# Attention steps of an encoder block: squares issued before the hi/lo split, small softmax steps on GpSimd, softmax scaling on ScalarE

## The chip, the cores and the metric

One core of a Trainium2 chip runs the kernel. The metric is the time of one launch on the device in microseconds; several runs give a median. One further execution is recorded by the hardware profiler, and the numbers of views come from it. The engines are PE (TensorE, matmuls), DVE (VectorE), ACT (ScalarE), POOL (GpSimd) and SP (SyncE, which here issues DMAs). Each works through its own list of instructions in order, and engines wait for each other through semaphores.

## The reference

One encoder layer over 256 tokens of width 2048, in float32. What matters here is the first half:

```
h = rmsnorm(x)
[q | k | v | u] = h @ w_in
# 12 query heads in 4 groups of 3, head width 128, window |t-s| <= 128
scores = q k^T * 128**-0.5 + alibi(slope of the head, |t-s|)
m = max(max_s scores, sink);  p = exp(scores - m)
p = p / (sum_s p + exp(sink - m));   a = p @ v
f = per group: Re(DFT2(u)) @ w_fourier
x = x + concat(rmsnorm(a), rmsnorm(f)) @ w_out
```

A feed-forward part with a width-3 convolution, GELU and a down-projection follows, and a final RMS norm. Nothing in it is touched.

## The kernel before

**Precision.** Every float32 factor is split into a coarse part (hi, made by a copy on ACT) and the rest (lo, a subtraction on DVE). A product is then three matmuls: hi by hi, hi by lo, lo by hi. Each weight tile of 128 x 2048 is split this way in `split` (lines 174 to 184), and the activations in `split_scaled` (267 to 272) and similar lines.

**Order.** The schedule is written out by hand: instructions stand on each engine in the order in which the Python code issues them. `unit(i, work)` (line 382) is one weight tile. It issues what is put `before` tile i (matmuls of the attention), the tile's own matmuls (`work`), what is put `beside` it (work of ACT, DVE and GpSimd on earlier results), then `split(i + 2)`, which makes the halves of the tile after next and issues the DMA that loads a further raw tile, then what is put `behind`. So TensorE runs tile i while ACT and DVE go through one round: the `beside` work, the split, the `behind` work. Three pairs of hi and lo buffers and three raw buffers rotate.

**Tiles.** Units 0 to 3 make u (for the Fourier part), 4 to 7 make v, 8 to 23 make the four key heads and twelve query heads in the order k, q, q, q (`QK_ORDER`), and 24 to 39 are the output projection. The feed-forward part has its own loop.

**Attention.** The loop of lines 762 to 791 spreads the steps of a head over the rounds. For the tile of slot s, in the round of unit
- s + 1: `qk_out` adds the two halves of the projection (`tmp` on ACT, `add` on DVE, for a key also a product with `r1b`), and `qk_parts` splits the sum into hi (ACT) and lo (DVE), the tiles `qT` and `kT`;
- s + 2: `scores` (six matmuls into `ps_s`, at the start of TensorE's part), then `scores_out` on DVE (add the distances and take the row maximum in one custom operation for each half; two steps on 128 x 2 elements give `neg`), and behind the split `exps` on ACT (exponentials with their row sums `sm`, and `ex`, the sink's term);
- s + 3: `weigh` (add the sink's term, reciprocal, scale the rows) and `flip_out` for the first ten heads (a 32 x 32 block transpose on DVE into `flip`, four DMAs on SP to `turnp` in HBM);
- s + 4: `flip_in`, the DMA back into `flop`; for the last two heads TensorE transposes instead (`turn`, `turn_out`);
- s + 6: `flip_parts`, hi and lo of the transposed weights (`pt`);
- s + 7 (s + 5 for the last two heads): `values` (six matmuls into `ps_o`) and `values_out`.

`values_out` and the Fourier part's last step call `feature_out`: it splits the scaled result into hi and lo (tile `cat`, the input of the output projection) and squares the unscaled result for the later RMS norm. The first square goes straight into the sum (`sq_a` or `sq_f`), the later ones into a scratch tile that GpSimd adds to it. GpSimd has little else in this stretch. The names `ps_...` are PSUM tiles; GpSimd takes no part with these.

In the round of unit i the order on each engine before the change is, where all steps occur:

```
ACT: pt hi | tmp | cat hi | square | kT/qT hi | split hi | exponentials, ex
DVE: pt lo | sm, reciprocal, 2 scalings | transpose | add | cat lo | kT/qT lo
     | 2 reductions, 2 neg steps | split lo
```

Of the kernel before, what the change touches and what calls it, by code (L numbers as in the profile page):

```python
# [8 lines left out]
F32 = mybir.dt.float32  # L9
F32R = mybir.dt.float32r  # L10
AF = mybir.ActivationFunctionType
ALU = mybir.AluOpType

P = 128
D = 2048
S = 256
# [88 lines left out]
def block_kernel(  # L105
# [19 lines left out]
    nc = tc.nc  # L125
# [3 lines left out]
    wp = ctx.enter_context(tc.tile_pool(name="wp", bufs=1))  # L129
# [3 lines left out]
    def f32(ap):  # L133
        return ap.bitcast(F32)

    def bank(pool, name):
        return pool.tile([P, 512], F32, tag=pool.name, name=name)
# [79 lines left out]
    def u_part(k, o, n, m=1):  # L217

        rows = ux[k // 4][:, (k < 4) * U_HEAD :].rearrange("p (k c) -> p k c", k=4)
        return rows[:, k % 4 : k % 4 + m, o : o + n]  # L220
# [39 lines left out]
    ps = bank(dn, "ps_warm")  # L260
# [3 lines left out]
    def vcol(o, n=1):  # L264
        return vec[:, o : o + n]

    def split_scaled(dst, src, g):

        nc.scalar.activation(dst[:, 0:S], src, AF.Copy, scale=g)
        nc.vector.scalar_tensor_tensor(  # L270
            dst[:, S : 2 * S], src, g, f32(dst[:, 0:S]), ALU.mult, ALU.subtract
        )
# [100 lines left out]
    before, beside, behind = {}, {}, {}  # L373

    def at(when, i, f, *a):
        when.setdefault(i, []).append((f, a))
# [17 lines left out]
    for k in range(NK):  # L394
# [7 lines left out]
        if q % n == 0:  # L402
            w, h = u_part(k, 0, FW, n), hi[:, q : q + n, :]
# [26 lines left out]
    rq_neg = ph.tile([P, 2], F32, tag="rq_neg", name="rq_neg")  # L430
    rq_pos = ph.tile([P, 2], F32, tag="rq_pos", name="rq_pos")
    rq_inv = ph.tile([P, 2], F32, tag="rq_inv", name="rq_inv")
    sink_neg = ph.tile([P, NH], F32, tag="sink_neg", name="sink_neg")
# [46 lines left out]
    def feature_out(ps, slot, g, sq, first):  # L480

        t = cat_pool.tile([P, 512], F32R, tag="cat", name=f"cat{slot}")
        split_scaled(t, ps, g)
        cat[slot] = t
        if first:
            nc.scalar.activation(sq, ps, AF.Square)
        else:
            one = wp.tile([P, 512], F32, tag="junk", name=f"sq{slot}")[:, 0:S]
            nc.scalar.activation(one, ps, AF.Square)
            nc.gpsimd.tensor_tensor(sq, sq, one, ALU.add)  # L490

    sums, r_af = {}, {}
# [91 lines left out]
    def fourier_channels_out(g):  # L584
        feature_out(held.pop(("y", g)), NH + g, vcol(V_GF + g), sq_f, g == 0)
# [43 lines left out]
    def qk_out(kind, h, ps):  # L629
        tmp = ph.tile([P, S], F32, tag="tmp", name=f"tmp_{kind}{h}", bufs=2)  # L630
        nc.scalar.activation(tmp, ps[:, S : 2 * S], AF.Copy)
        add = ph.tile([P, S], F32, tag="add", name=f"add_{kind}{h}", bufs=2)
        nc.vector.tensor_tensor(add, ps[:, 0:S], tmp, ALU.add)
        if kind == "k":
            nc.vector.tensor_tensor(add, add, r1b, ALU.mult)
        st["add", kind, h] = add
# [25 lines left out]
    def scores_out(h):  # L662

        ps = st.pop(("s", h))
        sc = ph.tile([P, 512], F32, tag="sc", name=f"sc{h}", bufs=4)
        mx = ph.tile([P, 2], F32, tag="mx", name=f"mx{h}", bufs=2)
        neg = ph.tile([P, 2], F32, tag="neg", name=f"neg{h}", bufs=2)
        for b in range(2):
            s = slice(b * S, (b + 1) * S)
            nc.vector.tensor_tensor_reduce(  # L670
                sc[:, s], ps[:, s], rel[:, s], -float(SL[h]), -3e38, ALU.add,
                ALU.max, mx[:, b : b + 1],
            )
        nc.vector.tensor_tensor(neg, mx, rq_neg, ALU.mult)
        nc.vector.tensor_scalar(neg, neg, sink_neg[:, h : h + 1], None, ALU.min)
        st["sc", h] = sc, neg

    def exps(h):
        sc, neg = st["sc", h]
        sm = ph.tile([P, 2], F32, tag="sm", name=f"sm{h}", bufs=2)  # L680
        ex = ph.tile([P, 2], F32, tag="ex", name=f"ex{h}", bufs=2)
        for b in range(2):
            s = slice(b * S, (b + 1) * S)
            nc.scalar.activation(
                sc[:, s], sc[:, s], AF.Exp, scale=rq_pos[:, b : b + 1],
                bias=neg[:, b : b + 1], accum_out=sm[:, b : b + 1],
            )
        nc.scalar.activation(ex, neg, AF.Exp, bias=vcol(V_SINK + h))
        st["sc", h] = sc, sm, ex

    def weigh(h):
        sc, sm, ex = st["sc", h]
        nc.vector.tensor_tensor(sm, sm, ex, ALU.add)
        nc.vector.reciprocal(ex, sm)
        for b in range(2):
            s = slice(b * S, (b + 1) * S)
            nc.vector.tensor_scalar(sc[:, s], sc[:, s], ex[:, b : b + 1], None, ALU.mult)

    def turn(h):
        ps = st["t", h] = bank(dn, f"ps_t{h}")  # L700
# [56 lines left out]
    def values_out(h):  # L757
        feature_out(st.pop(("o", h))[:, 0:S], h, vcol(V_GA + h), sq_a, h == 0)
# [3 lines left out]
    for i in range(N_QK, N_OUT + 8):  # L762
        heads = {i - s: h for (kind, h), s in slot_of.items() if kind == "q"}
        new = [kh for kh, s in slot_of.items() if i - s == 1]
        for n, h in sorted(heads.items()):
            if n == 5 + 2 * (h in FLIPS):
                at(before, i, values, h)
        if 4 in heads and heads[4] not in FLIPS:
            at(before, i, turn, heads[4])
        if 2 in heads:  # L770
            at(before, i, scores, heads[2])
        if 6 in heads and heads[6] in FLIPS:
            at(beside, i, flip_parts, heads[6])
        if 3 in heads:
            at(beside, i, weigh, heads[3])
            if heads[3] in FLIPS:
                at(beside, i, flip_out, heads[3])
        if 4 in heads and heads[4] in FLIPS:
            at(beside, i, flip_in, heads[4])
        for kind, h in new:  # L780
            at(beside, i, lambda k=kind, h=h: qk_out(k, h, st.pop(("ps", k, h))))
        for n, h in sorted(heads.items()):
            if n == 5 + 2 * (h in FLIPS):
                at(beside, i, values_out, h)
        if 4 in heads and heads[4] not in FLIPS:
            at(beside, i, turn_out, heads[4])
        for kind, h in new:
            at(beside, i, qk_parts, kind, h)
        if 2 in heads:
            at(beside, i, scores_out, heads[2])  # L790
            at(behind, i, exps, heads[2])

    fourier_channels_steps()
# [84 lines left out]
    for n, (c, kq) in enumerate(OUT_ORDER):  # L878
        i = N_OUT + n
# [14 lines left out]
        if kq >= 2:  # L894
            part = "a" if kq == 2 else "f"
            ps = ps_a[c] if kq < 3 else ps_a[c, "f"]
# [315 lines left out]
    for q in range(2):  # L1212
        kind, j = items[q]
        ps = bank(mm, f"ps_{kind}{j}")
# [15 lines left out]
    for n, it in enumerate(items):  # L1230
# [8 lines left out]
        if it[0] in ("gate", "val"):  # L1239
            kind, j = it  # L1240
            ps = bank(mm, f"ps_{kind}{j}")
# [4 lines left out]
        if it[0] == "product":  # L1246
# [4 lines left out]
            elif end and p in ("P2", "N4"):  # L1251
                ps = joined[c, p] = bank(mm, f"ps_{p}{g}{c}")
                by_parts(ps, parts[p], *halves.pop(it), GROUPS[g][1], True, False)
            else:
                ps = bank(mm, f"ps_{p}{g}{c}")
# [5 lines left out]
        else:  # L1261
            kind, c = it
            hi, lo = halves.pop(up_index[n])
            if c < 2:
                ps = [joined.pop((c, p)) for p in ("P2", "N4")]
            else:
                ps = [bank(mm, f"ps_l{c}{b}") for b in range(2)]
# [10 lines left out]
    i = up_index[n]  # L1278
# [37 lines left out]
    junk = wp.tile([P, 512], F32, tag="junk", name="junkc31")[:, 0:256]  # L1316
# [120 lines left out]
```

## Time and profile before

| | us |
|---|---|
| runs: median (lowest to highest) | 946.17 (945.48 to 946.81) |
| the profiled execution, its own time | 944.83 |
| its span in the trace | 943.0 |
| idle of ACT ahead of squares, waiting for DVE | 24.9 in 11 waits, 2.8 in one more |
| GpSimd busy | 50.8 |
| split of one weight tile: hi on ACT, lo on DVE | 1.90, 2.29 |

The profiled execution's time is 1.8 us more than its span: what lies before the first and after the last instruction. A line of a group or a timeline names the engine, the line of the kernel, the operation, output and inputs without buffer numbers, and the shapes; in brackets stands the idle time just before the instruction and what ended it. In the chain that ended last, each line is a start, a length and a piece of work; a piece that has been split over several lines is written as one. L697 DVE is a scaling, L314 the block transpose, L740 `pt` lo, L182 and L181 the split's lo and hi. Waits that are marked with another instruction's name are inferred from semaphores.

### The profile page before, as it was taken

How to read it: one execution, taken by the hardware profiler on the slowest of the kernel's cores; microseconds unless marked ns; L12 is line 12 of the kernel's file. 1: busy time of each engine (PE TensorE's matmuls, PEld its weight loads, DVE VectorE, ACT ScalarE, POOL GpSimd, SP SyncE). 2: the span in 40 equal slices, each digit the busy share in tenths (PEclk: the TensorE clock that was granted, in tenths of full speed). 3: DMA queues.
4: the chain of work that ended last, by engine and by line, in shares of the span. 5: the costliest groups of instructions: out<-in, count | busy, mean ns of one | idle time of the engine just before them, and what ended most of it. 6: DMA issues, size and time to landing. Idle time of an engine off the chain costs nothing.

```text
span 943.0 us, 12851 instructions
## 1 busy us (share of the span) xinstructions
PE 930.6 (99%) x5005; PEld 805.6 (85%) x5005; DVE 771.4 (82%) x981; ACT 540.5 (57%) x672; POOL 50.8 (5%) x68
## 2 busy tenths in 40 slices
PE   9999989999999999999999999999999999999996
PEld 7888878888888888888888888888888888888885
DVE  7658788777777878799887997878988779989986
ACT  7755566645554564566555565555655556655553
POOL 0100000100000000000000000000000000000002
PEclk9999989999999999999999999999999999999998
DMA  9965766566766578877798769787787878779652
GB/s 364 310 224 168 225 200 190 191 209 248 259 229 206 183 238 245 269 250 235 250 272 254 243 230 284 241 265 228 260 247 239 301 240 266 226 236 277 201 179 89
DMA packets 55149, 223.26 MB, mean 237 GB/s; under 512 B 21136, under 2 KB 25744, under 8 KB 31536
## 3 DMA queue, kind: packets, MB, share of 16 engines
q1 hardware_dynamic: 50544, 192.94, 56.6%
q0 software_dynamic: 4544, 29.49, 16.7%
q8 instruction: 39, 0.64, 0.3%
q14 instruction: 22, 0.18, 0.1%
HBM read 216.13 MB, written 6.29 MB: 236 GB/s over the span
## 4 chain that ended last, share of the span: by engine, by line
PE 88%; DVE 5%; ACT 4%; issue 2%; DMA 1%; DVEq 0%; SPq 0%; POOLq 0%; POOL 0%; ACTq 0%
PE ps_val L350 25%; PE ps_gate L350 25%; PE ps_P L1148 3%; PE ps_P L1146 3%; PE ps_P L1147 3%; PE ps_N L1148 3%; PE ps_N L1147 3%; PE ps_N L1146 3%; PE ps_a L335 2%; PE ps_a L334 2%; PE ps_a L333 2%; ACT hi L181 2%; DVE lo L182 1%; PE ps_ff L333 1%; PE ps_ff L335 1%
## 5 line engine op out<-in xcount | busy, mean ns | idle before, releaser
L182 DVE TENSOR_TENSOR lo<-raw,hi 128x2048 fp32r<-128x2048 f32 (+1 forms) x129 | 293.4, 2274 | 46.4 <-ACT hi L181 43.7
L181 ACT ACTIVATE hi<-raw 128x2048 fp32r<-128x2048 f32 (+1 forms) x129 | 245.2, 1901 | 34.2 <-PE ps_a L334 14.4
L350 PE MATMUL ps_val<-hU,hi 128*128 128x512 f32 x688 | 236.2, 389 | 0.0
L350 PE MATMUL ps_gate<-hU,hi 128*128 128x512 f32 x688 | 236.2, 389 | 0.0
L350 PE MATMUL ps_val<-hU,lo 128*128 128x256 f32 x688 | 189.9, 276 | 0.0
L350 PE MATMUL ps_gate<-hU,lo 128*128 128x256 f32 x688 | 189.9, 276 | 0.0
L350 PEld LDWEIGHTS ps_gate<-hU,hi 128*128 128x128 f32 x688 | 129.2, 188 | 26.8
L350 PEld LDWEIGHTS ps_val<-hU,hi 128*128 128x128 f32 x688 | 129.1, 188 | 26.8
L350 PEld LDWEIGHTS ps_gate<-hU,lo 128*128 128x128 f32 x688 | 129.2, 188 | 1.3
L350 PEld LDWEIGHTS ps_val<-hU,lo 128*128 128x128 f32 x688 | 129.2, 188 | 1.3
L921 ACT ACTIVATE ft_g<-ps_gate 128x256 f32<-128x256 f32 x43 | 16.5, 384 | 123.1 <-PE ps_gate L350 123.1
L921 ACT ACTIVATE ft_v<-ps_val 128x256 f32<-128x256 f32 x43 | 16.5, 384 | 91.8 <-PE ps_val L350 91.8
L350 PE MATMUL ps_q<-hT,hi 128*128 128x512 f32 x192 | 67.2, 401 | 0.0
L1146 PE MATMUL ps_P<-hi_P,op_P 128*128 128x512 f32 x144 | 56.0, 389 | 0.0
L1147 PE MATMUL ps_P<-hi_P,op_P 128*128 128x512 f32 x144 | 56.0, 389 | 0.0
L1148 PE MATMUL ps_P<-lo_P,op_P 128*128 128x512 f32 x144 | 56.0, 389 | 0.0
L350 PE MATMUL ps_q<-hT,lo 128*128 128x256 f32 x192 | 52.0, 281 | 0.0
L1038 DVE TENSOR_TENSOR lo_N<-sumw,hi_N 128x2048 fp32r<-128x2048 f32 (+1 forms) x20 | 41.5, 2076 | 9.4 <-ACT hi_N L1037 9.2
L350 PEld LDWEIGHTS ps_q<-hT,hi 128*128 128x128 f32 x192 | 36.3, 194 | 7.0
L1146 PE MATMUL ps_N<-hi_N,op_N 128*128 128x512 f32 x108 | 42.0, 389 | 0.0
L1147 PE MATMUL ps_N<-hi_N,op_N 128*128 128x512 f32 x108 | 42.0, 389 | 0.0
L1148 PE MATMUL ps_N<-lo_N,op_N 128*128 128x512 f32 x108 | 42.0, 389 | 0.0
(389 smaller groups left out, 1584.7 us busy)
## 6 DMA issues: line engine op xcount, KB each, us to landing
raw<-in_w_up SPq DMA_DIRECT2D x86, 1024.0 KB, 5.6
raw<-in_w_in SPq DMA_DIRECT2D x20, 1024.0 KB, 5.2
raw<-in_w_out SPq DMA_DIRECT2D x16, 1024.0 KB, 5.0
sumw<-in_w_down POOLq DMA_DIRECT2D x16, 1024.0 KB, 8.7
raw<-in_w_down_late SPq DMA_DIRECT2D x4, 1024.0 KB, 6.9
raw<-in_w_down_last SPq DMA_DIRECT2D x4, 768.0 KB, 4.2
turnp<-flip SPq DMA_DIRECT2D x40, 64.0 KB, 3.0
flop<-turnp SPq DMA_DIRECT2D x10, 256.0 KB, 4.0
```

Source lines behind the costliest of these rows:

```text
L181: nc.scalar.activation(hi[:, 0:n], raw[:, 0:n], AF.Copy)
L182: nc.vector.tensor_tensor(lo[:, 0:n], raw[:, 0:n], f32(hi[:, 0:n]), ALU.subtract)
L333: nc.tensor.matmul(ps, ah, wh, start=first and q == q0, stop=False)
L334: nc.tensor.matmul(ps, al, wh, start=False, stop=False)
L335: nc.tensor.matmul(ps, ah, wl, start=False, stop=last and q == q0 + len(kk) - 1)
L350: nc.tensor.matmul(ps[:, x], (hi, lo)[i][:, k * P : (k + 1) * P], hk(k)[:, x], start=n == 0 and k == 0, stop=n == len(order) - 1 and k == ...
L921: nc.scalar.activation(tmp, ps[:, S : 2 * S], AF.Copy)
L1038: nc.vector.tensor_tensor(lo, src, f32(hi), ALU.subtract)
L1146: nc.tensor.matmul(ps, o[:, 0, p, :], hi[:, s], start=first and p == 0, stop=False)
L1147: nc.tensor.matmul(ps, o[:, 1, p, :], hi[:, s], start=False, stop=False)
L1148: nc.tensor.matmul(ps, o[:, 0, p, :], lo[:, s], start=False, stop=last and p == n - 1)
```

## The change

Five edits, all in the attention stretch:

1. `feature_out` issues the square before the two instructions of the split; the GpSimd add of the scratch tile stays last.
2. The two 128 x 2 steps that make `neg` go from DVE to GpSimd.
3. The add of the sink's term to the row sums goes from DVE (start of `weigh`) to GpSimd (end of `exps`).
4. The two scalings of the softmax rows in `weigh` (128 x 256 each) go from DVE to ACT, as copies with a scale per partition.
5. In the loop, `scores_out` is put ahead of `qk_parts`, so that DVE's reductions stand before kT lo or qT lo.

```diff
@@ def feature_out(ps, slot, g, sq, first):
         t = cat_pool.tile([P, 512], F32R, tag="cat", name=f"cat{slot}")
+        one = sq
+        if not first:
+            one = wp.tile([P, 512], F32, tag="junk", name=f"sq{slot}")[:, 0:S]
+        nc.scalar.activation(one, ps, AF.Square)
         split_scaled(t, ps, g)
         cat[slot] = t
-        if first:
-            nc.scalar.activation(sq, ps, AF.Square)
-        else:
-            one = wp.tile([P, 512], F32, tag="junk", name=f"sq{slot}")[:, 0:S]
-            nc.scalar.activation(one, ps, AF.Square)
+        if not first:
             nc.gpsimd.tensor_tensor(sq, sq, one, ALU.add)
@@ def scores_out(h):
-        nc.vector.tensor_tensor(neg, mx, rq_neg, ALU.mult)
-        nc.vector.tensor_scalar(neg, neg, sink_neg[:, h : h + 1], None, ALU.min)
+        nc.gpsimd.tensor_tensor(neg, mx, rq_neg, ALU.mult)
+        nc.gpsimd.tensor_scalar(neg, neg, sink_neg[:, h : h + 1], None, ALU.min)
@@ def exps(h):
         nc.scalar.activation(ex, neg, AF.Exp, bias=vcol(V_SINK + h))
+        nc.gpsimd.tensor_tensor(sm, sm, ex, ALU.add)
@@ def weigh(h):
-        nc.vector.tensor_tensor(sm, sm, ex, ALU.add)
         nc.vector.reciprocal(ex, sm)
         for b in range(2):
             s = slice(b * S, (b + 1) * S)
-            nc.vector.tensor_scalar(sc[:, s], sc[:, s], ex[:, b : b + 1], None, ALU.mult)
+            nc.scalar.activation(sc[:, s], sc[:, s], AF.Copy, scale=ex[:, b : b + 1])
@@ the loop over units
+        if 2 in heads:
+            at(beside, i, scores_out, heads[2])
         for kind, h in new:
             at(beside, i, qk_parts, kind, h)
         if 2 in heads:
-            at(beside, i, scores_out, heads[2])
             at(behind, i, exps, heads[2])
```

The order in a full round after the change:

```
ACT: pt hi | 2 scalings | tmp | square | cat hi | kT/qT hi | split hi | exponentials, ex
DVE: pt lo | reciprocal | transpose | add | cat lo | 2 reductions | kT/qT lo | split lo
POOL: add of squares | 2 neg steps | sm
```

## The prediction

> **What bounds the kernel now.** I read the page first, then the chain that ended last in order of time, then the waits of each engine, then the timelines and windows of the stretch that these point to.
>
> ```profile
> PE 930.6 (99%) x5005; PEld 805.6 (85%) x5005; DVE 771.4 (82%) x981; ACT 540.5 (57%) x672; POOL 50.8 (5%) x68
> ```
>
> TensorE is busy nearly throughout, so only a stretch where it waits or runs at a lower clock can give time. The chain leaves TensorE for long only between 59 and 155 us, where it goes to and fro between ACT and DVE:
>
> ```profile
> 99.90 0.75 DVE pt L740 x2
> ...
> 113.39 0.75 DVE pt L740 x2
> 114.71 0.36 DVE sc L697
> 115.10 0.71 DVE flip L314
> 116.15 0.42 DVE add_k L635
> 116.58 0.41 DVE cat L270
> 117.06 0.39 ACT sq L489
> 117.75 1.82 ACT hi L181
> 119.60 2.29 DVE lo L182
> ...
> 155.90 5.47 PE ps_q L350 x32
> ```
>
> From 113.39 on this is one round: everything done beside a weight tile, then the two halves of a later tile (hi on ACT, lo on DVE). TensorE pays for the rounds in three places:
>
> ```profile
> 95.91 1.20 PE L654 MATMUL ps_s<-kT,qT 128*128 128x256 f32 x6
> 122.15 0.40 PE L350 MATMUL ps_q<-hT,lo 128*128 128x256 f32 x2
> 125.09 2.01 PE L654 MATMUL ps_s<-kT,qT 128*128 128x256 f32 x6 [2.54 <-ACT qT L269]
> 154.54 0.40 PE L654 MATMUL ps_s<-kT,qT 128*128 128x256 f32 x2
> 155.15 0.74 PE L654 MATMUL ps_s<-kT,qT 128*128 128x256 f32 x4 [0.22 <-DVE qT L270]
> ```
>
> ```profile
> 93.00:99.00 6.00, 5.87 (x35) 4.98 (x34) 4.10 (x10) 3.10 (x5) 0.72 (x1) 1.00 0.77 228
> 124.80:125.00 0.20, 0.00 (x0) 0.00 (x0) 0.00 (x0) 0.20 (x2) 0.19 (x1) 0.50 1.26 492
> 131.60:131.80 0.20, 0.20 (x3) 0.20 (x2) 0.17 (x3) 0.20 (x1) 0.00 (x0) 1.00 0.68 287
> ```
>
> In the windows the granted clock is the last column but two. The waits are 0.13 us near 96 (6.00 less 5.87), 2.54 up to 125.09, and 0.22 at 155. The long one also cools the clock: it stands at half from about 124.8 to 131.6, 6.8 us, which costs 3.4. Nothing else is to be won here: 0.13 + 2.54 + 3.4 + 0.22 = 6.3 us. All of it hangs on when three query tiles (qT) are ready; their hi halves start at 95.44, 124.63 and 153.90:
>
> ```profile
> 95.44 0.42 ACT L269 ACTIVATE qT<-add_q 128x256 fp32r<-128x256 f32 x1 [2.71 <-DVE add_q L633]
> 124.63 0.41 ACT L269 ACTIVATE qT<-add_q 128x256 fp32r<-128x256 f32 x1
> 153.90 0.41 ACT L269 ACTIVATE qT<-add_q 128x256 fp32r<-128x256 f32 x1
> ```
>
> **Squares ahead of the split, reductions ahead of the query halves.**
>
> ```profile
> ACT sq L489 <- DVE cat L270: 24.9, 11, 3.3
> 117.06 0.39 ACT L489 ACTIVATE sq<-ps_o 128x256 f32<-128x256 f32 x1 [3.32 <-DVE cat L270]
> 117.34 0.41 ACT L643 ACTIVATE kT<-add_k 128x256 fp32r<-128x256 f32 x1
> 117.79 0.76 DVE L644 TENSOR_TENSOR kT<-add_k,kT 128x256 fp32r<-128x256 f32 x1 [0.82 <-ACT kT L643]
> ```
>
> Today the square waits for DVE's cat half, and kT hi (or qT hi) and the whole ACT split stand behind the square. After the change the square and cat hi run on ACT while DVE transposes and adds, and the next thing ACT waits for is the add alone. In the round from 113.39 the add ends at 116.57 (116.15 + 0.42) and kT hi starts at 117.34. A hand-over costs 0.04 (kT hi ends at 117.75, kT lo starts at 117.79), so kT hi can start at 116.61, 0.73 earlier. I take 0.7 for every round in which this wait is on the chain: up to the third query three rounds from 105 to 129 and three from 135 to 158 (the wait occurs 11 times; the others come later). In the rounds before 99.90 the square reads SBUF, does not wait, and nothing is won. The reductions now stand ahead of kT lo, but DVE has to wait for ACT's hi there anyway.
>
> **Scaling on ACT.**
>
> ```profile
> 114.05 0.15 DVE L693 TENSOR_TENSOR sm<-sm,ex 128x2 f32<-128x2 f32 x1
> 114.24 0.17 DVE L694 RECIPROCAL ex<-sm 128x2 f32<-128x2 f32 x1
> 114.44 0.62 DVE L697 TENSOR_SCALAR sc<-sc,ex 128x256 f32<-128x256 f32 x2
> 73.46 0.49 ACT L269 ACTIVATE cat<-y,vec 128x256 fp32r<-128x256 f32 x1
> 73.86 0.40 ACT L489 ACTIVATE sq<-y 128x256 f32<-128x256 f32 x1
> ```
>
> From reciprocal to transpose DVE takes 0.86 today (114.24 to 115.10). The nearest ACT row is cat hi from SBUF with a scale per partition: 0.49, the next instruction 0.40 later. So a pair of scalings is 0.40 + 0.49 = 0.89, and with 0.17 for the reciprocal and two hand-overs the way takes 1.14. Bounds for the pair: 0.62 (DVE's price) and 1.05 (the second waits for the end of the first); I take 0.89, the row that it is nearest to. The sm add that leaves DVE gives back 0.19. Net +0.09 us in each round that weighs. While ACT waits for the reciprocal, tmp, square, cat hi, qT hi and the split stand behind it; DVE's transpose waits for ACT, and on SP the four turnp issues and the next raw load wait for the transpose. tmp and the square fit under the transpose (0.71), so only the +0.09 is on the chain.
>
> **Small steps on GpSimd.**
>
> ```profile
> L1323 POOL TENSOR_TENSOR ssq<-ssq 128x1 f32<-128x1 f32 x2 | 0.4, 192 | 1.2 <-ACT junkc L1165 0.9 <-ACT junkc L1317 0.3
> 35.48 2.29 DVE L182 TENSOR_TENSOR lo<-raw,hi 128x2048 fp32r<-128x2048 f32 x1
> 35.62 2.72 POOL L280 TENSOR_TENSOR rstd<-var,half_pow 128x2 f32<-128x2 f32 x1 [34.13 <-DVE var L277]
> 96.46 0.72 POOL L280 TENSOR_TENSOR rstdf<-varf,half_pow 128x2 f32<-128x2 f32 x1 [13.37 <-DVE varf L277]
> 120.97 0.28 ACT L688 ACTIVATE ex<-neg,vec 128x2 f32<-128x2 f32 x1
> 121.80 0.15 DVE L693 TENSOR_TENSOR sm<-sm,ex 128x2 f32<-128x2 f32 x1
> ```
>
> An add of one element costs 0.19 there. But the same operation on two elements took 0.72 alone and 2.72 when it began inside a DVE lo split; it ended 0.57 after that split (38.34 against 37.77). I read this as GpSimd held off until DVE lets go. The new sm add is released when ex ends (121.25), which always falls inside the lo split (119.60 to 121.89): ex ends 1.7 after hi, lo 2.3 after hi. So the sum ends about 0.2 after lo and the reciprocal starts some 0.3 later than it could. Bounds: 0 (not held) and 0.57; I take 0.28. The two neg steps cost the chain nothing if they end before lo starts. In the round from 113.39 lo would start near 119.2; cat lo would end near 117.4, the reductions by 118.4 (today they and neg fill the 1.05 from kT lo's end, 118.55, to lo), the two steps of 0.2 by 118.9. That margin of 0.3 is their cover; without it the third rival below is due.
>
> **The sum.** Each weighing round costs 0.09 + 0.28 = 0.37; where the square waited it gains 0.7, net -0.33. Three weighing rounds without that gain lie up to the first query: +1.1. Three with it lead to the second: +1.1 - 1.0 = +0.1. Three more to the third: -0.9. TensorE then waits 0.13 + 1.1 = 1.2 near 96, arrives at 122.55 + 1.1 = 123.65 for the second query and waits until 125.2, 1.5: the same idle time in two pieces. From there to the third query it needs 29.4 us today (125.09 to 154.54), 26.0 at a warm clock: it arrives at 151.2 and waits for a query that ends its hi half at 153.90 + 0.41 - 0.9 = 153.4. With the 0.22 that it waits today, that is 1.1 us won, set by the rounds and not by TensorE. If the first piece already cools the clock, TensorE reaches the third query at about 153.1, with the same end; if the second does, it arrives at 154.6 and wins nothing. I count no gain behind the third query. The profiled execution took 944.83, 1.34 less than the median of the runs: 943.7 there, **945.1** as a median.
>
> The Trainium skill, "TensorE: Matmul & The Clock Gate", section "Why this matters for your kernels", warns only of idle gaps above some 3 us. By it no wait of this sum would cool the clock and the 1.1 would be safe. The trace does not agree: it cooled some 2.2 us into a gap (122.55 to 124.8).
>
> **The rivals.**
>
> First, GpSimd is not held: the 2.72 is then a first-use cost, for that row is the first arithmetic on GpSimd in the trace. Against it: the operation ended right after lo. Each weighing round is 0.28 cheaper: +0.3 at the first query, -1.6 at the second, -3.4 at the third. TensorE waits 0.4 and 0.7, stays warm, reaches the third query at 149.5 and waits 1.4: 3.6 won, 942.6. The Trainium skill, "GPSIMD Engine Reference", section "2.1 Instruction dispatch", knows a first-call cost of about 6 us; the row's excess is 2.0.
>
> Second, slower: the third wait, 151.2 to 153.4, cools the clock. It is 2.2 us long, and as much was enough at 124.8. Then 3.4 are paid after a start that is 1.1 earlier: 2.3 slower, 948.5. It decides if neither of the two shorter waits has cooled it before.
>
> Third, slower: a neg step is caught by lo. The exponentials then start some 2.5 us late, and pt hi, pt lo and the scaling of the next round about 2. Four rounds up to the third query have both: +8 against -1.1, some 7 slower, 953. Against it stands the margin of 0.3.
>
> Fourth, the change does not do what it says: ACT is freed from one wait and put into another at the scaling. With the pair at 1.05 the nine weighing rounds lose 0.16 each, 1.4 in all, and 1.1 - 1.4 leaves 946.5.
>
> **How the numbers follow.** Forecast and fourth rival have 0.32 between them, the forecast the larger part; first rival 0.24, second 0.27, third 0.13, something faster that I do not see 0.04. What a measurement of this kernel tells from no change is about 0.2%, 1.9 us. The forecast splits into 0.22 same, 0.07 faster, 0.03 slower, as the bounds of its prices shift it by 1 to 2 us; first rival and the unseen are faster, 0.28; the second 0.21 slower, 0.06 same; the third slower. So faster 0.35, same 0.28, slower 0.37. The range goes from 941.5 (the first rival, a little better) to 951.0, which leaves most of the third out; the forecast's own range is 943 to 947.
>
> **What would show it.** Right: no ACT square waiting for a DVE cat; GpSimd sm adds that end just after a lo split; reciprocals 0.3 late behind it; TensorE waiting 1.2, 1.5 and 2.2 us at the scores. Wrong: sm adds over in 0.2 while lo runs (first rival); half clock after 153 (second); exponentials that start only after lo ends (third). A pair of ACT scalings above 1.1 us, or new waits of TensorE outside 60 to 160 us, would make the sum wrong.

## The result, and the profile after

The changed kernel takes 943.01 us as a median (942.31 to 943.97), against 946.17 for the kernel before, measured beside it. The ratio is 0.9968 (0.9957 to 0.998): 3.2 us, or 0.32%, faster. The profiled execution took 942.31, 2.5 less than that of before.

The busy time of the engines, from the page of the changed kernel:

```profile
PE 927.9 (99%) x5005; PEld 802.7 (85%) x5005; DVE 756.1 (80%) x921; ACT 550.7 (59%) x696; POOL 70.7 (8%) x104
```

Work moved as the edits say: DVE is 15.3 us less busy, ACT 10.2 more, GpSimd 19.9 more. That is no explanation of the time yet, since TensorE sets the end. TensorE's timeline shows the six score matmuls of the three queries, with the idle time ahead of them in brackets:

```profile
96.61 1.20 PE L654 MATMUL ps_s<-kT,qT 128*128 128x256 f32 x6 [0.76 <-ACT qT L269]
124.40 1.21 PE L654 MATMUL ps_s<-kT,qT 128*128 128x256 f32 x6 [1.15 <-ACT qT L269]
152.18 1.20 PE L654 MATMUL ps_s<-kT,qT 128*128 128x256 f32 x6 [1.12 <-ACT qT L269]
```

The waits sum to 3.03 us. Before they were 0.13, 2.54 and 0.22, 2.89 in all. So TensorE idles as long as ever, only in three pieces. What it won stands in the windows between the scores of the second query and the end of TensorE's work ahead of the third (columns: length, TensorE busy, granted clock, DMA share, GB/s), first of the kernel before:

```profile
125.05:154.50 29.45, 29.41 (x164) 0.89 0.63 200
```

and the same 164 matmul records of the changed kernel:

```profile
124.36:151.02 26.66, 26.62 (x164) 1.00 0.68 207
```

The stretch at half clock is gone, and the same work takes 2.79 us less. 2.79 + 2.89 - 3.03 = 2.65 is what the third query should gain; its last four score matmuls began at 155.15 before, and begin at 152.58 now (152.18 plus the 0.40 that the first two take), 2.57 earlier. The span is 2.5 shorter, so nothing was won or lost behind that point.

That the long wait broke into short ones is the work of the rounds on ACT and DVE. ACT's timeline gives the start of hi of the three query tiles:

```profile
96.14 0.42 ACT L269 ACTIVATE qT<-add_q 128x256 fp32r<-128x256 f32 x1 [0.82 <-DVE add_q L633]
123.93 0.42 ACT L269 ACTIVATE qT<-add_q 128x256 fp32r<-128x256 f32 x1 [0.19 <-DVE add_q L633]
151.71 0.42 ACT L269 ACTIVATE qT<-add_q 128x256 fp32r<-128x256 f32 x1 [0.18 <-DVE add_q L633]
```

From query to query four rounds (three of which weigh) take 27.79 and 27.78 us; before it was 29.19 and 29.27. These two intervals are the measure used below, because they don't depend on when the trace begins. TensorE itself needs 26.66 for an interval.

### The profile page after: what moved, and what is told of

The parts are those of the page before. It is cut to its first block, busy times and chain, and to the rows that moved or that the text cites. A ratio compares the mean times of both kernels' runs of the same rounds, so it can differ in the third digit from the quotient of the medians.

```text
span 940.5 us, 12840 instructions
## 1 busy us (share of the span) xinstructions
PE 927.9 (99%) x5005; PEld 802.7 (85%) x5005; DVE 756.1 (80%) x921; ACT 550.7 (59%) x696; POOL 70.7 (8%) x104
## 4 chain that ended last, share of the span: by engine, by line
PE 88%; ACT 4%; DVE 3%; issue 3%; DMA 1%; POOL 0%; DVEq 0%; SPq 0%; POOLq 0%; ACTq 0%
PE ps_val L350 25%; PE ps_gate L350 25%; PE ps_P L1147 3%; PE ps_P L1148 3%; PE ps_P L1149 3%; PE ps_N L1147 3%; PE ps_N L1148 3%; PE ps_N L1149 3%; PE ps_a L335 2%; PE ps_a L333 2%; PE ps_a L334 2%; ACT hi L181 2%; ACT sc L697 1%; PE ps_ff L333 1%; PE ps_ff L335 1%
## 5 line engine op out<-in xcount | busy, mean ns | idle before, releaser
L350 PE MATMUL ps_q<-hT,hi 128*128 128x512 f32 x192 | 65.1, 391 | 0.0
```

Source lines behind the costliest of these rows:

```text
L350: nc.tensor.matmul(ps[:, x], (hi, lo)[i][:, k * P : (k + 1) * P], hk(k)[:, x], start=n == 0 and k == 0, stop=n == len(order) - 1 and k == ...
```

## The experiments

Two theories. **A**: the squares' new place gives the whole gain, and each step that left DVE costs a little. **B**: DVE was the bound and the gain comes from relieving it. Later a third joined, **L**: GpSimd and DVE hold each other off for whole instructions, and which of the two comes first decides what an edit costs. All ratios are to the kernel before, measured beside each (946.17 for the change, 945.5 for e1 to e14); an interval is from one query's hi to the next, from ACT's timeline.

| kernel | median us | ratio (95% interval) | intervals us |
|---|---|---|---|
| before | 946.17 | 1 | 29.19, 29.27 |
| the change | 943.01 | 0.9968 (0.9957 to 0.998) | 27.79, 27.78 |
| e1 squares only | 943.75 | 0.9981 (0.9972 to 0.999) | 28.17, 28.71 |
| e2 change, squares back | 948.13 | 1.003 (1.0019 to 1.0042) | 29.64, 29.63 |
| e3 change, sm add back on DVE | 944.35 | 0.999 (0.9981 to 0.9999) | 28.25, 28.26 |
| e4 change, scalings back on DVE | 940.98 | 0.9954 (0.9941 to 0.9968) | 27.21, 27.48 |
| e6 squares only, no GpSimd adds | 940.34 | 0.995 (0.9938 to 0.9963) | 27.07, 27.07 |
| e7 change, lo in two parts | 942.91 (one run) | | 27.87, 27.86 |
| e8 change, neg steps back on DVE | 943.41 | 0.9974 (0.9964 to 0.9983) | 27.77, 27.79 |
| e9 change, reductions back | 942.39 | 0.997 (0.9958 to 0.9982) | 27.78, 27.78 |
| e12 e4, ten square adds on DVE | 939.84 | 0.9938 (0.9926 to 0.9951) | 26.67, 26.65 |
| e13 e4, all square adds on DVE | 939.33 | 0.9935 (0.9921 to 0.9948) | 26.67, 26.67 |
| e14 e9, neg 0.3 later | 964.40 | 1.0196 (1.0183 to 1.021) | 33.57, 33.55 |

**The squares alone (e1), and everything but the squares (e2).** e1 is the kernel before with the first edit; e2 is the changed kernel with that edit undone:

```diff
-        one = sq
-        if not first:
-            one = wp.tile([P, 512], F32, tag="junk", name=f"sq{slot}")[:, 0:S]
-        nc.scalar.activation(one, ps, AF.Square)
         split_scaled(t, ps, g)
         cat[slot] = t
-        if not first:
+        if first:
+            nc.scalar.activation(sq, ps, AF.Square)
+        else:
+            one = wp.tile([P, 512], F32, tag="junk", name=f"sq{slot}")[:, 0:S]
+            nc.scalar.activation(one, ps, AF.Square)
             nc.gpsimd.tensor_tensor(sq, sq, one, ALU.add)
```

> The kernel before with the squares alone moved ahead of the split; reductions, small steps and scalings as before. Theory A: the whole gain of the change comes from the squares (0.72 us in each of the six weighing rounds in which the square waited), and the work that left VectorE costs 0.15 to 0.28 a round. Then the first query stays at 95.44 us, the second comes near 122.4, so that TensorE waits 0.3 to 0.5 there instead of 2.54, the clock stays at 1.0, and the third comes near 149.6 with a wait of some 0.5: about 4.5 us ahead of the kernel before, 941.7 as a median, 1.3 faster than the whole change. Theory B: the gain comes from VectorE being relieved (its busy time fell by 15 us); then this kernel gains less than 1 us and stays above 945.

> The changed kernel with the squares put back behind the split; everything else as in the change. Theory A: the first query stays at 96.14, the second comes 3 x 0.72 later than in the changed kernel, near 126.1; TensorE, there at 123.25, waits about 3.3, the clock drops to half for one stretch (2.8 us), and the third query comes near 156, 1.5 to 2.5 later than in the kernel before: 947.5 to 948.7 as a median, slower than before. Theory B: most of the gain stays, 943 to 944.5.

e2 came out as A expects: without the squares the rest of the change is a loss, 948.13. TensorE's wait and clock in e2, from its waits (total, times, longest) and a window:

```profile
PE ps_s L654 <- ACT qT L269: 5.3, 3, 3.0
```

```profile
128.00:130.00 2.00, 2.00 (x9) 0.50 0.71 182
```

A wait of 3.0 and a stretch at half clock, as before the change. So B is out. But e1 missed: 943.75 and not 941.7. The first interval won 1.02 where 2.2 was expected, the second 0.56. Timelines of GpSimd and DVE in e1 show where it went:

```profile
113.43 1.02 POOL L490 TENSOR_TENSOR sq_a<-sq_a,sq 128x256 f32<-128x256 f32 x1 [15.89 <-ACT sq L486]
```

```profile
113.09 0.75 DVE L740 TENSOR_TENSOR pt<-flop,pt 128x256 fp32r<-128x256 f32 x2
113.76 0.70 DVE L693 TENSOR_TENSOR sm<-sm,ex 128x2 f32<-128x2 f32 x1
114.50 0.17 DVE L694 RECIPROCAL ex<-sm 128x2 f32<-128x2 f32 x1
```

The square is now done early, so GpSimd's add of it is issued at 113.43, while DVE makes pt lo. It ends at 114.45, 0.61 after the row of pt lo (113.84); alone it takes 0.72 to 0.74. DVE's sm add, which took 0.15 in the kernel before, takes 0.70 and ends with it. That is theory L: each waits out the other's whole instruction. In the first interval two of the three sm adds are long, in the second all three; 0.55 each makes 1.1 and 1.65, which is what is missing.

**The GpSimd adds taken out of e1 (e6).**

```diff
-        if not first:
+        if not first and sq is not sq_a:
             nc.gpsimd.tensor_tensor(sq, sq, one, ALU.add)
```

> The kernel with only the squares moved, and in it the nine adds on GpSimd that sum the squares of the attention heads left out (that sum is then missing). Theory L (lock): VectorE and GpSimd hold each other off for whole instructions; with only the squares moved, the GpSimd add begins right behind pt lo or the lo split and holds VectorE's sm add for 0.70 instead of 0.15. Without the adds the sm adds are 0.15 again in all 12 rounds; four of them lie before the third query, so it comes 4 x 0.55 earlier, near 150.5, and the kernel takes about 941.5 as a median, 2.2 less than with the squares alone. Theory R: the long sm adds are a matter of VectorE's own order; then nothing moves, 943.5 to 944.

The adds left out are eleven, one for each head but the first, and not nine. The intervals fell by 1.10 and 1.64, the very sums of the held sm adds, and the group of sm adds is short again in all twelve rounds:

```profile
L693 DVE TENSOR_TENSOR sm<-sm,ex 128x2 f32<-128x2 f32 x12 | 1.8, 152 | 0.0
```

The time fell by more than expected (940.34 against 941.5): five rounds before the third query were held and not four, and e1 had a stretch at half clock that e6 has not. So the squares give 2.1 to 2.2 an interval, 0.71 to 0.73 in each of three rounds, once nothing is in their way.

**One step at a time back to DVE (e3, e4, e8).** Each undoes one edit of the change. e3, the sm add, from `exps` back to `weigh`:

```diff
-        nc.gpsimd.tensor_tensor(sm, sm, ex, ALU.add)
+        nc.vector.tensor_tensor(sm, sm, ex, ALU.add)
```

e4, the two scalings:

```diff
-            nc.scalar.activation(sc[:, s], sc[:, s], AF.Copy, scale=ex[:, b : b + 1])
+            nc.vector.tensor_scalar(sc[:, s], sc[:, s], ex[:, b : b + 1], None, ALU.mult)
```

e8, the two neg steps:

```diff
-        nc.gpsimd.tensor_tensor(neg, mx, rq_neg, ALU.mult)
-        nc.gpsimd.tensor_scalar(neg, neg, sink_neg[:, h : h + 1], None, ALU.min)
+        nc.vector.tensor_tensor(neg, mx, rq_neg, ALU.mult)
+        nc.vector.tensor_scalar(neg, neg, sink_neg[:, h : h + 1], None, ALU.min)
```

> The changed kernel with the sm add back on VectorE, ahead of the reciprocal. Theory A, GpSimd is held off only until the lo split ends: the reciprocal comes 2.39 us after the start of lo as it does now in rounds where it follows lo directly, and 0.19 later in rounds where pt lo stands between; of the six weighing rounds between the first and the third query four are such, so the third query comes 0.8 later, 943.8 as a median. The forecast's size of the hold (0.28 in every round): 0.09 is won in each of nine rounds, 0.8 in all, 942.2.

> The changed kernel with the two scalings back on VectorE (sum and neg steps stay on GpSimd). Theory A: the way from reciprocal to transpose is 0.86 again instead of 1.14 to 1.19, so each weighing round is 0.3 shorter; first query near 95.2, second near 122.2, third near 149.1, and TensorE's waits fall from 3.0 us to about 0.5: 2.5 us faster than the change, 940.5 as a median. Theory B (VectorE must be relieved): 0.62 us of work go back to VectorE in each round, and it comes out slower than the change, 944 or more.

> The changed kernel with the two neg steps back on VectorE, behind the reductions. Theory H (hidden): on either engine they end before hi does, and VectorE waits 0.9 for hi there anyway; the queries come within 0.2 of where they do now and the time is that of the change, 942.4 to 943.5. Theory B (VectorE must be relieved): 0.39 of work goes back to VectorE in each round and delays lo by up to 0.4: 1 us or more slower, 944 or more.

All three came out as A (e3, e4) and H (e8) expect, within 0.6. With the sm add on DVE an interval is 0.46 longer (e3; 0.4 was expected): it is better off on GpSimd, though held there. With the neg steps on DVE it is the same (27.77, 27.79): they are hidden on either engine. With the scalings on DVE it is shorter by 0.58 and 0.30 (e4), so moving them to ACT was a loss. Of A's steps that left DVE, only the scalings cost anything: the sm add paid, and the neg steps did neither. The ways (1.14 to 1.19 against 0.86) give an estimate of 0.3 a round, 0.9 an interval. Part of it is lost to another hold, seen in e4's timelines of GpSimd and DVE:

```profile
112.98 1.01 POOL L490 TENSOR_TENSOR sq_a<-sq_a,sq 128x256 f32<-128x256 f32 x1 [0.20 <-ACT sq L486]
```

```profile
113.51 0.89 DVE L697 TENSOR_SCALAR sc<-sc,ex 128x256 f32<-128x256 f32 x2
```

The pair of scalings takes 0.89 in place of 0.62 where the square's add on GpSimd (to 113.99) overlaps it.

**The lo split cut in two (e7).** If GpSimd gets its turn when the DVE instruction in progress ends, a cut in that instruction should let it in:

```diff
-        nc.vector.tensor_tensor(lo[:, 0:n], raw[:, 0:n], f32(hi[:, 0:n]), ALU.subtract)
+        cuts = [0, 1536, n] if N_QK <= i < N_OUT + 8 and n == 2048 else [0, n]
+        for a, b in zip(cuts, cuts[1:]):
+            nc.vector.tensor_tensor(lo[:, a:b], raw[:, a:b], f32(hi[:, a:b]), ALU.subtract)
```

> The changed kernel with the lo split of the query and key stage cut into two VectorE instructions, 1536 and 512 columns. Theory L: GpSimd gets its turn when the VectorE instruction in progress ends. The sm add, which begins 1.4 us after lo does, then ends just after the first part (some 1.8 after the start) and takes about 0.45 instead of 0.94, and the reciprocal comes within 0.1 of the end of the second part, at most 0.1 later than now. Theory R: the add is slow for a reason of its own (two elements per partition, its first operand from ScalarE); it stays at 0.94 and ends in the middle of the second part.

From e7's timelines of DVE (both parts in one row) and GpSimd, and the group of the first part (busy, mean ns of one):

```profile
111.40 2.36 DVE L184 TENSOR_TENSOR lo<-raw,hi 128x1536 fp32r<-128x1536 f32 x2 [0.87 <-ACT hi L181]
```

```profile
112.81 0.41 POOL L691 TENSOR_TENSOR sm<-sm,ex 128x2 f32<-128x2 f32 x1 [1.85 <-ACT ex L690]
```

```profile
L184 DVE TENSOR_TENSOR lo<-raw,hi 128x1536 fp32r<-128x1536 f32 x10 | 17.6, 1758 | 11.4 <-ACT hi L181 11.4
```

The first part ends at 111.40 + 1.76 = 113.16, the sm add at 113.22, with 0.5 of lo still to come. So GpSimd is let in at the end of an instruction, not at the end of the work. The intervals are 0.08 longer, but not evenly: three of the four rounds take 0.06 or 0.07 more, the price of one more DVE instruction, and the one in which no pt lo stands ahead of the reciprocal takes 0.11 less (6.73 in place of 6.84). There the reciprocal no longer waits for the sm add, by e7's timeline of DVE:

```profile
119.44 2.36 DVE L184 TENSOR_TENSOR lo<-raw,hi 128x1536 fp32r<-128x1536 f32 x2 [0.88 <-ACT hi L181]
121.72 0.16 DVE L696 RECIPROCAL ex<-sm 128x2 f32<-128x2 f32 x1
```

It starts 2.28 after lo, though lo is 0.07 longer; in the change it starts 2.38 after.

**The reductions back (e9), and the margin of the neg steps taken away (e14).** e9 undoes the fifth edit; e14 adds to e9 a repeated first neg step:

```diff
-        if 2 in heads:
-            at(beside, i, scores_out, heads[2])
         for kind, h in new:
             at(beside, i, qk_parts, kind, h)
         if 2 in heads:
+            at(beside, i, scores_out, heads[2])
             at(behind, i, exps, heads[2])
```

```diff
-        nc.gpsimd.tensor_tensor(neg, mx, rq_neg, ALU.mult)
+        for _ in range(2):
+            nc.gpsimd.tensor_tensor(neg, mx, rq_neg, ALU.mult)
```

> The changed kernel with the reductions back behind the query or key halves on VectorE. The reductions end 0.4 later, so the second neg step ends 0.1 or less before the lo split starts: the forecast's margin of 0.3 is used up. Theory M (the margin decides): where the second step is caught by lo it ends with lo, the exponentials start 2.3 us late, and the kernel is 3 us or more slower than the change, 946 or more. Theory N: the steps slip in ahead of lo (lo waits for ScalarE's hi, which does not move), and the time is the same as the change within 0.5, 942.5 to 943.5.

> The kernel with the reductions back behind the halves, and the first neg step issued twice with the same result, so that the last neg step begins about 0.3 later. In the former its second step ended 0.04 before lo began (119.16 against 119.20). Theory M: now that step falls inside lo, is held to its end (about 2.3 later), and the exponentials, which wait for it, start 2.3 late; the sums come 1.5 or more late in each of the rounds that weigh, and TensorE waits over 3 us at the second query: 948 to 957. Theory N: a step that is released while GpSimd is already at work is not held; 0.3 a round at most, 942.5 to 944.5.

The last neg step of a round in the changed kernel, from GpSimd's timeline; lo starts at 119.35 there:

```profile
118.62 0.28 POOL L675 TENSOR_SCALAR neg<-neg,sink_neg 128x2 f32<-128x2 f32 x1
```

It has 0.45 to spare. In e9 it just slips in ahead of lo (GpSimd, then DVE):

```profile
118.88 0.28 POOL L675 TENSOR_SCALAR neg<-neg,sink_neg 128x2 f32<-128x2 f32 x1
```

```profile
119.20 2.29 DVE L182 TENSOR_TENSOR lo<-raw,hi 128x2048 fp32r<-128x2048 f32 x1 [0.70 <-ACT hi L181]
```

It ends at 119.16, 0.04 before lo starts, and the time is that of the change. The new place of the reductions is worth nothing as such; it is what makes the margin. In e14 the step comes 0.3 later, and GpSimd, DVE and ACT read:

```profile
125.70 2.40 POOL L676 TENSOR_SCALAR neg<-neg,sink_neg 128x2 f32<-128x2 f32 x1
```

```profile
125.75 2.29 DVE L182 TENSOR_TENSOR lo<-raw,hi 128x2048 fp32r<-128x2048 f32 x1 [0.69 <-ACT hi L181]
```

```profile
128.14 0.60 ACT L685 ACTIVATE sc<-sc,neg,rq_pos 128x256 f32<-128x256 f32 x1 [2.43 <-POOL neg L676]
```

Begun at 125.70, 0.05 ahead of lo, it is held all the same and ends at 128.10, just after lo (128.04). The exponentials wait 2.43 for it, an interval becomes 33.57, and the kernel takes 964.4, above even the 957 that Theory M allowed. So 0.3 us on GpSimd cost 22 us, the steepest edge that these runs show.

**A kernel without the two losses (e12, e13).** The scalings go back to DVE, and the add of the attention squares goes from GpSimd to DVE, behind the key or query halves, where DVE waits for hi:

```diff
+            if sq is sq_a:
+                add_square()
...
-        if not first:
+        if not first and sq is sq_a:
+            ones_of.append(one)
+        elif not first:
             nc.gpsimd.tensor_tensor(sq, sq, one, ALU.add)
+
+    ones_of = []
+
+    def add_square():
+        while ones_of:
+            nc.vector.tensor_tensor(sq_a, sq_a, ones_of.pop(0), ALU.add)
...
             at(beside, i, qk_parts, kind, h)
+        at(beside, i, add_square)
```

The scalings' lines, as in e4, are left out here. e12 keeps only one pending square; as two heads end in one late round, one of the eleven adds is missing from its sum. e13 has all of them.

> The changed kernel with the scalings back on VectorE and the add that sums the attention squares moved from GpSimd to VectorE, behind the query or key halves, where VectorE waits 0.9 to 1.4 us for hi. Theory L: with the scalings on VectorE that add began right behind the sm add and held the first scaling for 0.38 (pair 0.89 instead of 0.62 to 0.70) in four rounds before the third query; now the pair takes 0.62 again, the third query comes up to 1.0 earlier, bounded by TensorE's remaining waits of 0.57 and 0.75, and the kernel takes 940.0, 1 us less than with the scalings back alone. Theory R: nothing moves, 941.0; if the add delays lo, more.

> The changed kernel with the scalings back on VectorE and the adds of the attention squares on VectorE behind the query or key halves, all eleven of them. The run with ten of them had TensorE waiting for next to nothing at the three queries and took 939.84; the eleventh stands after the third query, so this takes 939.5 to 940.3, and is 2.8 to 3.4 us faster than the change. If the eleventh is on the chain, or the time was a matter of the missing one, 941 or more.

e13's timeline of DVE, the scalings and the add in its gap ahead of lo:

```profile
113.13 0.62 DVE L707 TENSOR_SCALAR sc<-sc,ex 128x256 f32<-128x256 f32 x2
...
116.59 0.41 DVE L500 TENSOR_TENSOR sq_a<-sq_a,sq 128x256 f32<-128x256 f32 x1
117.55 2.29 DVE L182 TENSOR_TENSOR lo<-raw,hi 128x2048 fp32r<-128x2048 f32 x1 [0.54 <-ACT hi L181]
```

and two windows of it (columns as above), where TensorE waits for 0.05 us and for nothing, and stays at full clock:

```profile
120.00:128.00 8.00, 7.95 (x47) 1.00 0.71 213
...
150.00:155.00 5.00, 5.00 (x31) 1.00 0.79 195
```

The intervals are 26.67, TensorE's own need. 939.33 is 6.1 us faster than before in its own comparison (945.47), about twice the gain of the change and a little below the 939.5 expected, and there is next to nothing left to win at the three queries.

## Why the prediction came out as it did

The time lies inside the range, 2.1 below the forecast: 3.2 us were won where 1.1 was forecast, three times as much. The result stands at the edge of the forecast's own range (943 to 947); the wider range went below that for the first rival, whose reason turned out wrong, so that part of its cover was luck. The direction of the forecast held, though its chances had put slower (0.37) a little above faster (0.35). The place (the three queries), the squares as the largest term and "no gain behind the third query" held too. The steps one by one:

- **Squares, 0.7 a round.** Right. In the changed kernel kT hi starts 0.04 after the add's end and not 0.77; e6 gives 0.71 to 0.73 a round.
- **Scaling on ACT, way 0.86 to 1.14, pair 0.89.** Right: the pair takes 0.91, the way 1.14 in a round without pt (121.73 to 122.87 below) and 1.19 in one with it. e4 shows that the edit is a loss, as its sign in the sum says.
- **GpSimd held off by lo, reciprocal 0.28 later in every round.** The mechanism held, the size was wrong, and this is the step that failed. GpSimd's and DVE's timelines of the changed kernel:

```profile
120.75 0.94 POOL L689 TENSOR_TENSOR sm<-sm,ex 128x2 f32<-128x2 f32 x1 [1.84 <-ACT ex L688]
```

```profile
111.38 2.29 DVE L182 TENSOR_TENSOR lo<-raw,hi 128x2048 fp32r<-128x2048 f32 x1 [0.88 <-ACT hi L181]
113.59 0.75 DVE L740 TENSOR_TENSOR pt<-flop,pt 128x256 fp32r<-128x256 f32 x2
114.27 0.16 DVE L694 RECIPROCAL ex<-sm 128x2 f32<-128x2 f32 x1
...
119.35 2.29 DVE L182 TENSOR_TENSOR lo<-raw,hi 128x2048 fp32r<-128x2048 f32 x1 [0.88 <-ACT hi L181]
121.73 0.17 DVE L694 RECIPROCAL ex<-sm 128x2 f32<-128x2 f32 x1
122.87 0.71 DVE L314 STREAM_TRANSPOSE flip<-sc 128x512 f32<-128x512 f32 x1 [0.98 <-ACT sc L697]
```

  The sm add does end with lo: 121.69 against 121.64. But 0.05 behind it is not 0.2. After lo DVE's next instruction can start 2.21 after lo began (113.59 less 111.38); the reciprocal starts 2.38 after (121.73 less 119.35), so the hold costs 0.17. And where pt lo stands first, as in four of the six rounds between the first and the third query, the sum is ready before the reciprocal's turn, and the hold costs nothing at all. The forecast charged 0.28 nine times. A round thus won 0.44 to 0.58 (from one key or query hi to the next, in the first interval: 7.91 to 7.39, 8.41 to 7.97, 7.29 to 6.84), not 0.33 (ACT's timelines). e7, where the hold ends early, bears out the 0.17: the reciprocal starts 2.28 after lo there, which is 2.21 and the 0.07 by which that lo is longer.
- **The first three weighing rounds, +1.1.** They cost 0.63 (0.07 of the 0.70 by which the query comes later is there at the first key already): 0.10 in the round in which other work precedes the reciprocal, 0.26 and 0.27 in the others, in place of 0.37 each.
- **TensorE's waits of 1.2, 1.5 and 2.2.** They are 0.76, 1.15 and 1.12. The first two are shorter for the same reason; of the third, 0.6 is TensorE's own work between the queries, 26.66 in place of 26.0, which is the next term. The long third wait of the second rival did not arise, so it was not tried whether 2.2 would have cooled the clock there.
- **The clock, 3.4.** The stretch cost 2.79, not half of 6.8: it began 0.36 before the matmuls did, and under it a matmul pair took less than double (0.64 in place of 0.34).
- **First rival, GpSimd not held.** Its time (942.6) is nearest to the result, but its reason is wrong: e7 and e14 show the hold. The right number for the wrong reason is why the sm adds had to be looked at and not the time alone.
- **Third rival, a neg step caught by lo.** It did not occur, with a margin of 0.45 for the 0.3 worked out. The mechanism is real and was under-priced: e14 pays 22 us against e9 where the rival had 8, as ten of the twelve steps are hit (2.40 to 2.43 each) and the clock cools besides (its mean is 0.71 from 131 to 140 us).
- **What was in no step.** The adds of the squares on GpSimd. They held DVE in the kernel before already, by its timelines of GpSimd and DVE:

```profile
154.08 0.74 POOL L490 TENSOR_TENSOR sq_a<-sq_a,sq 128x256 f32<-128x256 f32 x1 [6.54 <-ACT sq L489]
```

```profile
154.34 0.76 DVE L270 SCALAR_TENSOR_TENSOR qT<-add_q,qT 128x256 fp32r<-128x256 f32 x1 [0.82 <-ACT qT L269]
```

  The third query's lo takes 0.76 here and 0.42 in the changed kernel; the 0.34 covers the whole 0.22 that TensorE waited. The kT lo of 0.76 at 117.79, in the prediction's own lines, is another such row. The place of the adds changes with edit 1, and in five of the six rounds they lengthen DVE's work by 0.26 to 0.29 in e4 and by 0.55 in e1, and by 0.12 in the key rounds of the changed kernel (add_k takes 0.54 for 0.42). What takes them out of the way of the sm add in the change is edit 4: the squares stand behind the scalings on ACT, so their adds start later. In e3, with the sm add on DVE and the scalings on ACT, it takes 0.16 again (DVE, then GpSimd):

```profile
115.30 0.16 DVE L693 TENSOR_TENSOR sm<-sm,ex 128x2 f32<-128x2 f32 x1
```

```profile
117.29 0.74 POOL L490 TENSOR_TENSOR sq_a<-sq_a,sq 128x256 f32<-128x256 f32 x1 [5.31 <-ACT sq L486]
```

Most of the 2.1 is two things: the rounds' part is 1.3 at the third query (153.0 forecast, 151.71 measured). Another 0.6 is the way from a profiled execution to a median: 1.34 was taken over from before, and it is 0.70 here.

The Trainium skill, "SBUF — State Buffer", section "Who interferes with whom", states that a VectorE instruction with two inputs in SBUF and a GpSimd instruction that reads SBUF shut each other out for a whole instruction, whichever comes first. The runs agree in both directions: the sm add on GpSimd ends 0.05 after lo, and DVE's sm add in e1 takes 0.70 in place of 0.15. That rule, applied to the squares' adds too, would have given an sm add that ends with lo, and the collisions of e1. The scalings held in e4 have one tensor as input, so the rule as told here doesn't cover them. In e14 a step whose row begins 0.05 ahead of lo was held all the same, so which comes first can't be read from the rows to that accuracy.

## What to carry to other kernels

Before work moves to GpSimd, list what DVE runs at the moment of its release, and who waits for each of the two: a two-element step cost 0.2, 0.94 or 2.4 us here by that alone. An edit that frees an engine earlier also releases what waits behind it, and that can land on the chain elsewhere (e1's squares gave a half and a quarter of what they could in the two intervals, until the adds behind them were left out). Undo each edit of a bundle by itself: here one paid 1.85 us an interval, one 0.46, two nothing, and one took back 0.3 to 0.6.

## What the runs showed of the hardware that was not expected

An instruction of GpSimd that began, by its row, 0.05 us before a DVE instruction was still held for all of it (e14: 125.70 and 125.75). In e9 one that began 0.32 before was not (118.88 and 119.20); it had ended 0.04 before the DVE instruction began.

The clock did not follow the length of the wait alone. In e1 TensorE waited 1.53 and fell to half clock at about 125.8, 1.4 us after that wait had ended; in e3 it waited 1.63 and did not. TensorE's timeline and a window behind it, of e1:

```profile
124.44 1.20 PE L654 MATMUL ps_s<-kT,qT 128*128 128x256 f32 x6 [1.53 <-ACT qT L269]
```

```profile
126.00:128.00 2.00, 2.00 (x8) 0.50 0.90 226
```

and of e3:

```profile
125.72 1.20 PE L654 MATMUL ps_s<-kT,qT 128*128 128x256 f32 x6 [1.63 <-ACT qT L269]
```

```profile
126.00:128.00 2.00, 2.00 (x13) 1.00 1.06 323
```

A wait of 1.15 in the changed kernel was not followed by a drop, nor were e2's first (1.27) and e3's first (1.37). What decides near 1.5 stays open; it wasn't tried. It matters for reading small differences, since a drop cost up to 2.8 us at the second query, nearly as much as the whole change won.
